# The latent queries' DRAM scratch, split into two tensors: nope rows and rotary rows of all heads

## The chip, the cores and the metric

One NeuronCore of a Trainium2 chip runs the whole kernel in one launch. The metric is device time in microseconds (us) of one execution; lower is better. The program runs on one core, so there is one span and one TensorE clock to look at.

Names of engines: PE is TensorE (PEld its weight loads), DVE is VectorE, ACT is ScalarE, POOL is GpSimd, SP is SyncE. SP computes nothing here: it issues most of the DMAs, strictly in its own order. ACT also issues some DMAs, in between its computing. "SPq" and "ACTq" are these two issuing sequencers.

## The reference, cut to what matters

One layer of an encoder is applied to two groups of tokens (2048 and 512) with the same weights. Only branch B, the latent attention, is touched. Its queries come from a latent vector of 384 values per token and fall into a part without position (nope, 64 values per head) and a rotary part (32 values per head), for 8 heads:

```python
q = (rms_norm(cq, g_q) @ w_uq).reshape(B, S, B_HEADS, NOPE_DIM + ROPE_DIM)
q_nope, q_rope = q[..., :NOPE_DIM], q[..., NOPE_DIM:]
...
q_rope = apply_rope(q_rope, cos[:, None, :], sin[:, None, :])
...
q = jnp.concatenate([q_nope, q_rope], axis=-1) * scale
...
s = jnp.einsum("bqhd,bkhd->bhqk", q_blk, k)
p = jax.nn.softmax(s, axis=-1)
o = jnp.einsum("bhqk,bkhd->bqhd", p, v)
```

Everything is float32. The kernel keeps the precision on TensorE by splitting each value into a high part and a low part, so that each matrix product becomes three matmuls.

## The kernel before, in words

The tokens are cut into NC = 5 chunks of T = 512 (chunks 0 to 3 are the long group, chunk 4 the short one). The program has three stages, and data passes from one to the next through scratch tensors in DRAM.

**Stage one** (to about 590 us) makes, chunk by chunk, all projections that attention needs. In `chunk` (from L376), round a and round b multiply the normed tokens by the weight columns of the latents (tiles `tka`, `tkb`); then four `qa_` steps make the windowed branch's queries, with the transposes of the next chunk's tokens (`pt`, L251) and its `hh` tiles (`h_tile`, ACT at L260, DVE at L257 and L261) between them; then the latents are transposed (`ct`, L491). What makes the latent queries, keys and values of the chunk is the list of closures of `heads` (L300): `qr_`, `kn_`, `qn_`, `v_` four times each, then `qrt_` twice. This list is not run at once: it is kept as `late` and dealt out between the matmuls of rounds a and b of the next chunk. The last chunk's list runs at the end of the stage, with three of its `qa_` steps between.

Each of these steps puts its result into a tile of the tag `ev`, of which there are EV = 6: 128 partitions by 2 (high, low) by 512 values, 512 KB. ACT writes the high half, DVE the low half, then SP stores the tile to DRAM. `qn_` (L328) holds the nope rows of two heads and stores them at L340; `qrt_` (L363) holds the rotary rows of four heads and stores them at L372. Both go to `q_d[c]` (L78), which has for each head 96 rows: 64 nope rows, then 32 rotary rows, each row 4 KB. A `qn` store thus writes two separate blocks of 64 rows, and a `qt` store four separate blocks of 32 rows:

```python
nc.sync.dma_start(q_d[c][2 * j:2 * j + 2, 0:64], f(qn))
...
nc.sync.dma_start(q_d[c][4 * i:4 * i + 4, 64:96], f(qt))
```

An `ev` tile can be written again only when its store has landed. `qa`, `kn`, `vt`, `krt` and `ka` tiles share the six buffers. With its 20 `qn` stores and 10 `qt` stores the kernel writes all of `q_d`. Late in the stage `first_max` (L271) reads back two heads' queries and takes row maxima with the matmuls `mq`, so that the first two items of stage two have theirs already.

**Stage two** (to about 1400 us) is the latent attention. Its 40 items are (head, chunk) pairs, laid out in units of one key block pair by a table (`at`, `run`, from L775); the order on PE, ACT, DVE and POOL is that of the table, while SP's order is set by the tile scheduler. `q_load` (L665) loads an item's 96 rows of queries into one of four `Q` tiles with one DMA (L668). Then the first matmuls `mp` of the item (L677) take its row maxima, and the matmuls `s` (L715 to L717) make its scores. `k_tile`, `load_k` and `load_v` load keys and values.

**Stage three** (to the end) is the windowed attention, the gates and the output projections. It does not read the latent queries.

The order of all instructions in stages one and three, and of SP everywhere, comes from a scheduler that runs when the program is built. A DMA of another shape can therefore move other instructions.

Of the kernel before, what the change touches and what calls it, by code (L numbers as in the profile page):

```python
# [9 lines left out]
F32 = mybir.dt.float32  # L10
# [8 lines left out]
P = 128  # L19
D = 1024  # L20
KD = D // P
T = 512
NS = 4
NC = 5
HA = 8
HB = 8
# [7 lines left out]
def f(ap):  # L34
    return ap.bitcast(F32)
# [3 lines left out]
def encoder(ctx: ExitStack, tc: tile.TileContext, x_prompt, x_sample, c_prompt, c_sample, b_ada, g_norm, g_q,  # L39
            w_uq, g_kv, w_ukv, sink, g_final, t_mod, t_gate, t_col, t_a, t_b, t_oa, t_ob, t_out, rope_c, rope_s, bias, sel, y_prompt, y_sample):  # L40
    nc = tc.nc
# [12 lines left out]
    dram = ctx.enter_context(tc.tile_pool(name="dram", bufs=1, space=DRAM))  # L54
# [5 lines left out]
    def pa(name):  # L60
        return pps["a"].tile([P, 512], F32, name=name, tag="a")

    def px(tag, name):
        return pps["t" if tag == "t0" else "c"].tile([P, 512], F32, name=name, tag=tag)
# [10 lines left out]
    bcol = const.tile([P, 2, KD], F32, name="bcol")  # L75

    h_d = [[dram.tile([P, 2, T], F32, name=f"h_d{c}_{k}") for k in range(KD // 2)] for c in range(NC)]
    q_d = [dram.tile([HB, 96, 2, T], F32, name=f"q_d{c}") for c in range(NC)]  # L78
    k_d = [dram.tile([HB, 64, 2, n * T], F32, name=f"k_d{n}") for n in (NS, 1)]
    kr_d = [dram.tile([32, 2, n * T], F32, name=f"kr_d{n}") for n in (NS, 1)]  # L80
    v_d = [dram.tile([HB, P, 4 * n, P], F32, name=f"v_d{n}") for n in (NS, 1)]
# [16 lines left out]
    def mm3(ps, wh, wl, mh, ml, first, last):  # L98
        nc.tensor.matmul(ps, wh, mh, start=first, stop=False)  # L99
        nc.tensor.matmul(ps, wl, mh, start=False, stop=False)  # L100
        nc.tensor.matmul(ps, wh, ml, start=False, stop=last)  # L101
# [105 lines left out]
    with psum("ps1a", 4) as pps["a"], psum("ps1t", 1) as pps["t"], psum("ps1c", 1) as pps["c"], \  # L207
# [5 lines left out]
        def tl(tag, shape, dt, name, bufs):  # L213
            return p1.tile(shape, dt, name=name, tag=tag, bufs=bufs)

        def tr(tag, shape, dt, name, bufs):
            return env["pl1"].tile(shape, dt, name=name, tag=tag, bufs=bufs)
# [54 lines left out]
        def first_max():  # L272
            K, Q = [], tl("hh", [P, 2, T], F32R, "qm", NH)
            for i in range(2):
                kt = tl("hh", [P, 2, T], F32R, f"km{i}", NH)
                for r0, src in ((0, k_d[0][0]), (64, kr_d[0])):
                    nc.sync.dma_start(f(kt[r0:r0 + src.shape[0]]).rearrange("p a b -> p (a b)"),
                                      src[:, 0, i * 1024:(i + 1) * 1024])
                K.append(kt)
            for c in range(NP):  # L280
                nc.sync.dma_start(f(Q[0:96, c]), q_d[c][0][:, 0, :])
            m0 = [tl("m0", [P, 4, 4], F32, f"m0_{c}", 2) for c in range(NP)]

            def step(c, i):
                ps = px(("t1", "t2", "t3")[i % 3], f"mq{c}_{i}")
                nc.tensor.matmul(ps, Q[0:96, c, i // 4 * P:(i // 4 + 1) * P], K[i % 4 // 2][0:96, i % 2],
                                 start=True, stop=True)
                nc.vector.tensor_reduce(out=m0[c][:, i // 4, i % 4:i % 4 + 1], in_=ps, axis=AX.X, op=ALU.max)

            def close(c):  # L290
                ng = tl("ng", [P, 4], F32, f"ng_{c}", 2)
                nc.vector.tensor_reduce(out=ng, in_=m0[c], axis=AX.X, op=ALU.max, negate=True)
                pt = px("t1", f"mr{c}")
                nc.tensor.transpose(pt[0:4, 0:P], ng, ident)
                rw = tl("rw", [4, P], F32R, f"rw_{c}", 2)
                nc.scalar.copy(rw, pt[0:4, 0:P])
                nc.sync.dma_start(rw_d[c][0], f(rw))

            out = []
            for c in range(NP):  # L300
                out += [lambda c=c, i=i: step(c, i) for i in range(16)] + [lambda c=c: close(c)]
            return out

        def heads(c, C):
            g, cg = c // NS, c % NS
            blk0 = cg * 4
            cs = slice(cg * T, (cg + 1) * T)
            qrs = []

            def ps_of(name):  # L310
                if c == NC - 1:
                    return pa(name)
                env["turn"] = env.get("turn", 0) + 1
                return px(("t0", "t1", "t2", "t3")[env["turn"] % 4], name)

            def ev_of(name):
                return tr("ev", [P, 2, T], F32R, name, EV)

            def qr_(t):
                ts = slice(t * P, (t + 1) * P)  # L320
                ps = ps_of(f"qr{c}_{t}")
                for k in range(3):
                    mm3(ps[:, 0:256], C[k][:, 0, ts], C[k][:, 1, ts], wuh[:, k, 512:768], wul[:, k, 512:768],
                        k == 0, k == 2)
                qs = tr("qs", [P, 8, 32], F32, f"qs{c}_{t}", 1)
                nc.scalar.activation(qs.rearrange("p h e -> p (h e)"), ps[:, 0:256], AF.Copy, scale=SB)
                qr = tr("qrr", [P, 8, 32], F32, f"qr{c}_{t}", 4)
                rope(qr, qs, 8, blk0 + t, f"q{c}_{t}")  # L328
                qrs.append(qr)

            def qn_(j):
                ps = ps_of(f"qn{c}_{j}")
                js = slice(j * P, (j + 1) * P)
                for k in range(3):
                    mm3(ps, wuh[:, k, js], wul[:, k, js], C[k][:, 0, :], C[k][:, 1, :], k == 0, k == 2)
                qn = ev_of(f"qn{c}_{j}")
                nc.scalar.activation(qn[:, 0, :], ps, AF.Copy, scale=SB)
                nc.vector.scalar_tensor_tensor(out=qn[:, 1, :], in0=ps, scalar=SB, in1=f(qn[:, 0, :]),
                                               op0=ALU.mult, op1=ALU.subtract)
                nc.sync.dma_start(q_d[c][2 * j:2 * j + 2, 0:64], f(qn))  # L340

            def kn_(j):
                ps = ps_of(f"kn{c}_{j}")
                js = slice(j * P, (j + 1) * P)
                for k in range(2):
                    mm3(ps, wkh[:, k, js], wkl[:, k, js], C[3 + k][:, 0, :], C[3 + k][:, 1, :], k == 0, k == 1)
                kn = ev_of(f"kn{c}_{j}")
                nc.scalar.copy(kn[:, 0, :], ps)
                nc.vector.tensor_tensor(out=kn[:, 1, :], in0=ps, in1=f(kn[:, 0, :]), op=ALU.subtract)
                nc.sync.dma_start(k_d[g][2 * j:2 * j + 2, :, :, cs], f(kn))  # L350

            def v_(t):
                ts = slice(t * P, (t + 1) * P)
                ps = ps_of(f"v{c}_{t}")
                for k in range(2):
                    mm3(ps, C[3 + k][:, 0, ts], C[3 + k][:, 1, ts], wkh[:, k, 512:1024], wkl[:, k, 512:1024],
                        k == 0, k == 1)
                vt = ev_of(f"vt{c}_{t}").rearrange("p a b -> p (a b)").rearrange("p (h e) -> p h e", h=HB)
                pv = ps.rearrange("p (h e) -> p h e", e=64)
                nc.scalar.copy(vt[:, :, 64:128], pv)  # L360
                nc.vector.tensor_tensor(out=vt[:, :, 0:64], in0=pv, in1=f(vt[:, :, 64:128]), op=ALU.subtract)
                nc.sync.dma_start(v_d[g][:, :, 4 * cg + t, :].rearrange("h p e -> p h e"), f(vt))

            def qrt_(i):
                pt = ps_of(f"qrt{c}_{i}")
                for t in range(4):
                    nc.tensor.transpose(pt[:, t * P:(t + 1) * P],
                                        qrs[t][:, 4 * i:4 * i + 4, :].rearrange("p h e -> p (h e)"), ident)
                qt = ev_of(f"qt{c}_{i}")
                nc.scalar.copy(qt[:, 0, :], pt)  # L370
                nc.vector.tensor_tensor(out=qt[:, 1, :], in0=pt, in1=f(qt[:, 0, :]), op=ALU.subtract)
                nc.sync.dma_start(q_d[c][4 * i:4 * i + 4, 64:96], f(qt))  # L372

            out = []
            for j in range(4):
                out += [(qr_, j), (kn_, j), (qn_, j), (v_, j)]  # L376
            return [lambda fn=fn, j=j: fn(j) for fn, j in out + [(qrt_, 0), (qrt_, 1)]]

        def chunk(c, H, nxt):
# [67 lines left out]
            if c == NC - 1:  # L447
                fm += first_max()
# [190 lines left out]
    with psum("ps2s", 2) as pss, psum("ps2v", 1) as ps2v, psum("ps2", 1) as ps2, pool("p2k") as pk, pool("p2q") as pq, pool("p2a") as p2a, \  # L639
# [25 lines left out]
        def q_load(it):  # L665
            nm = it.nm
            it.Q = pq.tile([97, 2, T], F32R, name=f"Q{nm}", tag="Q", bufs=4)
            nc.sync.dma_start(f(it.Q[0:96]), q_d[it.c][it.h])  # L668
            it.mx = pq.tile([P, 4, 2], F32, name=f"mx{nm}", tag="mx", bufs=5)
            it.ng = pq.tile([P, 4], F32, name=f"ng{nm}", tag="ng", bufs=5)  # L670

# [101 lines left out]
        it = items[0]  # L773
# [335 lines left out]
```

## Time and profile before

| | |
|---|---|
| median of 3 runs | 2773.03 us (2768.88 to 2774.62) |
| the profiled execution's own time | 2767.52 us |
| its span | 2765.6 us |
| mean granted TensorE clock | 0.973 of full speed |
| PE busy | 2589.5 us, 94% of the span |
| DVE, ACT, POOL busy | 61%, 49%, 60% |
| moved by DMA | 392.34 MB, mean 142 GB/s |

The profile shows one execution. In its rows a time is in us from the start of the span, and `x20` means 20 such instructions. "ACT qa L475 <- DMA q_d<-qt" reads: ACT stood still before the instruction at line 475 that writes `qa`, and what let it go was the landing of a DMA from `qt` to `q_d`. A DMA issue (`DMA_DIRECT2D`) on SPq has a duration of its own, the time that it held the issuing sequencer; its data can land much later. "DMA share" is the mean busy share of the core's 16 DMA engines, so that one engine busy all the time counts 0.06.

### The profile page before, as it was taken

How to read it: one execution, taken by the hardware profiler on the slowest of the kernel's cores; microseconds unless marked ns; L12 is line 12 of the kernel's file. 1: busy time of each engine (PE TensorE's matmuls, PEld its weight loads, DVE VectorE, ACT ScalarE, POOL GpSimd, SP SyncE). 2: the span in 40 equal slices, each digit the busy share in tenths (PEclk: the TensorE clock that was granted, in tenths of full speed). 3: DMA queues.
4: the chain of work that ended last, by engine and by line, in shares of the span. 5: the costliest groups of instructions: out<-in, count | busy, mean ns of one | idle time of the engine just before them, and what ended most of it. 6: DMA issues, size and time to landing. Idle time of an engine off the chain costs nothing. (4 is left out here: it accounts for less than half of the span.)

```text
span 2765.6 us, 33922 instructions
## 1 busy us (share of the span) xinstructions
PE 2589.5 (94%) x11842; PEld 2056.5 (74%) x11842; DVE 1691.2 (61%) x2507; ACT 1345.7 (49%) x2125; POOL 1647.4 (60%) x1012
## 2 busy tenths in 40 slices
PE   7998798967999999999899999999999999999998
PEld 4876686745777777777667787787788778778876
DVE  4544443526999999999957466537653754465325
ACT  4534343225777777777654444444344444443422
POOL 3544353316888888888774366436743773467345
PEclk9998899988999999999999999999999999999999
DMA  8557565454322232221245455434543563455341
GB/s 317 183 179 221 181 203 167 143 162 138 91 64 78 71 92 62 84 75 55 82 155 169 136 181 175 149 123 154 195 144 114 180 217 120 137 174 190 107 155 53
DMA packets 198360, 392.34 MB, mean 142 GB/s; under 512 B 17015, under 2 KB 96312, under 8 KB 196587
## 3 DMA queue, kind: packets, MB, share of 16 engines
q1 hardware_dynamic: 185138, 353.31, 39.3%
q10 hardware_dynamic: 13050, 36.86, 4.1%
q8 instruction: 93, 1.52, 0.2%
q14 instruction: 79, 0.64, 0.1%
HBM read 286.52 MB, written 103.58 MB: 141 GB/s over the span
## 5 line engine op out<-in xcount | busy, mean ns | idle before, releaser
L732 POOL TENSOR_TENSOR pl<-pf,ph 128x1024 fp32r<-128x1024 f32 x272 | 655.0, 2412 | 172.4 <-ACT pf L725 172.1
L122 POOL TENSOR_TENSOR wlgm<-wrgm,whgm 128x1024 fp32r<-128x1024 f32 x80 | 195.0, 2443 | 317.9 <-ACT whgm L121 226.0
L724 ACT ACTIVATE ph<-s 128x1024 fp32r<-128x1024 f32 x272 | 278.8, 1025 | 211.7 <-PE s L717 210.7
L683 DVE TENSOR_REDUCE mx<-mp 128x1 f32<-128x1024 f32 x240 | 292.7, 1220 | 56.4 <-PE mp L677 54.4
L745 DVE TENSOR_TENSOR ac<-ac,pf 128x512 f32<-128x512 f32 x424 | 294.2, 694 | 16.5 <-ACT pf L725 9.5
L725 ACT ACTIVATE pf<-s 128x1024 f32<-128x1024 f32 x272 | 275.8, 1014 | 0.0
L100 PE MATMUL gm<-H,wlgm 128*128 128x512 f32 x640 | 252.7, 395 | 0.0
L99 PE MATMUL gm<-H,whgm 128*128 128x512 f32 x640 | 251.8, 397 | 0.0
L101 PE MATMUL gm<-H,whgm 128*128 128x512 f32 x640 | 251.7, 394 | 0.0
L715 PE MATMUL s<-Q,K 97*128 97x512 f32 x544 | 217.6, 400 | 22.4 <-DMA k_d<-kn 22.3
L716 PE MATMUL s<-Q,K 96*128 96x512 f32 x544 | 217.3, 400 | 0.0
L717 PE MATMUL s<-Q,K 96*128 96x512 f32 x544 | 215.8, 397 | 0.0
L677 PE MATMUL mp<-K,Q 96*128 96x512 f32 x512 | 163.1, 400 | 25.3 <-DMA Q<-q_d 17.4
L757 PE MATMUL a<-ph,V 128*128 128x512 f32 x544 | 175.1, 403 | 0.1
L760 PE MATMUL a<-pl,V 128*64 128x512 f32 x544 | 170.7, 395 | 1.0 <-POOL pl L732 0.9
L166 DVE CUSTOM_DVE_ANT_0 S<-as,mask,snk 128x384 f32<-128x384 f32 (+1 forms) x160 | 89.2, 586 | 100.3 <-PE as L164 72.9
L677 PEld LDWEIGHTS mp<-K,Q 96*128 96x128 f32 x512 | 94.1, 190 | 64.8 <-DVE mx L683 18.3
L99 PEld LDWEIGHTS gm<-H,whgm 128*128 128x128 f32 x640 | 119.9, 188 | 25.6 <-issue 2.6
L715 PEld LDWEIGHTS s<-Q,K 97*128 97x128 f32 x544 | 103.4, 190 | 47.9 <-issue 22.5
L101 PEld LDWEIGHTS gm<-H,whgm 128*128 128x128 f32 x640 | 120.8, 189 | 24.5
L100 PEld LDWEIGHTS gm<-H,wlgm 128*128 128x128 f32 x640 | 120.8, 189 | 23.8
L187 DVE TENSOR_TENSOR PT<-pT,PT 128x512 fp32r<-128x512 f32 x112 | 77.1, 688 | 97.9 <-ACT PT L186 96.8
(259 smaller groups left out, 6643.6 us busy)
## 6 DMA issues: line engine op xcount, KB each, us to landing
wrgm<-in_t_col_dram SPq DMA_DIRECT2D x80, 512.0 KB
wrz<-in_t_col_dram SPq DMA_DIRECT2D x40, 512.0 KB
wrw<-in_t_out_dram SPq DMA_DIRECT2D x40, 512.0 KB
Q<-q_d SPq DMA_DIRECT2D x40, 384.0 KB
wrqa<-in_t_col_dram ACTq DMA_DIRECT2D x20, 512.0 KB
qa_d<-qa SPq DMA_DIRECT2D x40, 256.0 KB
k_d<-kn SPq DMA_DIRECT2D x20, 512.0 KB
q_d<-qn SPq DMA_DIRECT2D x20, 512.0 KB
```

What stands on the lines that cost most here:

```text
L99: nc.tensor.matmul(ps, wh, mh, start=first, stop=False)
L100: nc.tensor.matmul(ps, wl, mh, start=False, stop=False)
L101: nc.tensor.matmul(ps, wh, ml, start=False, stop=last)
L677: nc.tensor.matmul(ps[:, j, :], Q[0:96, 0, qt * P:(qt + 1) * P], K[0:96, 0, kc * T:(kc + 1) * T], start=True, stop=True)
L683: nc.vector.tensor_reduce(out=it.mx[:, i // 2, i % 2:i % 2 + 1], in_=it.mp.rearrange("p a b -> p (a b)"), axis=AX.X, op=ALU.max)
L715: nc.tensor.matmul(ps[:, j, :], K[0:97, 0, ks], Q[0:97, 0, :], start=True, stop=False)
L716: nc.tensor.matmul(ps[:, j, :], K[0:96, 1, ks], Q[0:96, 0, :], start=False, stop=False)
L717: nc.tensor.matmul(ps[:, j, :], K[0:96, 0, ks], Q[0:96, 1, :], start=False, stop=True)
L724: nc.scalar.activation(ph, it.s, AF.Exp)
L725: nc.scalar.activation(pf, it.s, AF.Exp)
L732: nc.gpsimd.tensor_tensor(out=pl, in0=it.pf[p], in1=f(it.ph[p]), op=ALU.subtract)
L745: nc.vector.tensor_tensor(out=sm if last and j else it.acc, in0=it.acc, in1=pf[:, j], op=ALU.add)
```

## The change

The scratch tensor `q_d` of each chunk becomes two: `qn_d` has the nope rows of all eight heads (512 rows), `qr_d` the rotary rows of all eight (256 rows). A `qn` store now writes 128 rows that follow each other, and so does a `qt` store. The bytes written and read are the same. The reader now needs two loads where there was one: 64 nope rows and 32 rotary rows, in `q_load` and in `first_max`.

```diff
-    q_d = [dram.tile([HB, 96, 2, T], F32, name=f"q_d{c}") for c in range(NC)]
+    qn_d = [dram.tile([HB * 64, 2, T], F32, name=f"qn_d{c}") for c in range(NC)]
+    qr_d = [dram.tile([HB * 32, 2, T], F32, name=f"qr_d{c}") for c in range(NC)]
...
             for c in range(NP):
-                nc.sync.dma_start(f(Q[0:96, c]), q_d[c][0][:, 0, :])
+                nc.sync.dma_start(f(Q[0:64, c]), qn_d[c][0:64, 0, :])
+                nc.sync.dma_start(f(Q[64:96, c]), qr_d[c][0:32, 0, :])
...
-                nc.sync.dma_start(q_d[c][2 * j:2 * j + 2, 0:64], f(qn))
+                nc.sync.dma_start(qn_d[c][j * P:(j + 1) * P], f(qn))
...
-                nc.sync.dma_start(q_d[c][4 * i:4 * i + 4, 64:96], f(qt))
+                nc.sync.dma_start(qr_d[c][i * P:(i + 1) * P], f(qt))
...
             it.Q = pq.tile([97, 2, T], F32R, name=f"Q{nm}", tag="Q", bufs=4)
-            nc.sync.dma_start(f(it.Q[0:96]), q_d[it.c][it.h])
+            nc.sync.dma_start(f(it.Q[0:64]), qn_d[it.c][it.h * 64:(it.h + 1) * 64])
+            nc.sync.dma_start(f(it.Q[64:96]), qr_d[it.c][it.h * 32:(it.h + 1) * 32])
```

The order of PE's instructions is the same through stages one and two. SP's order is the same in stage one but for the doubled loads. The first place to see is SP at the hand-over from stage one to stage two, where the last stores of chunk 4 and the first loads of keys (`K`) and queries (`Q`) meet (`rw_d` holds the row maxima of `first_max`). Before:

```order
L340 DMA q_d_94<-qn_2_5270 2x64x1024
L362 DMA v_d_100<-vt_2_5281 128x8x128
L647 DMA K_0_5428<-ones_d 1x2048
L649 DMA K_0_5428<-kr_d_97 32x4096
L655 DMA K_0_5428<-k_d_95 64x4096
L668 DMA Q_0_5432<-q_d_90 96x1024
L708 DMA Q_0_5432<-rw_d_136 1x512
```

and with the change:

```order
L342 DMA qn_d_94<-qn_2_5277 128x1024
L364 DMA v_d_105<-vt_2_5288 128x8x128
L649 DMA K_0_5435<-ones_d 1x2048
L651 DMA K_0_5435<-kr_d_102 32x4096
L657 DMA K_0_5435<-k_d_100 64x4096
L670 DMA Q_0_5439<-qn_d_90 64x1024
L671 DMA Q_0_5439<-qr_d_95 32x1024
L711 DMA Q_0_5439<-rw_d_141 1x512
```

The store has another shape (2 blocks of 64 rows became 128 rows), the query load is two rows, and the key loads stand behind the same store as before. The second place is SP in the middle of stage two, at the query load of chunk 3, where a store and a load of row maxima (`rw_d`) of other items stand around it. Before:

```order
L708 DMA Q_1_6115<-rw_d_137 1x512
L668 DMA Q_1_6582<-q_d_93 96x1024
L704 DMA rw_d_140<-rw_1_6493 4x128
L708 DMA Q_1_6319<-rw_d_140 1x512
L747 DMA sm_d_126<-sm_1_6504 128x512
```

and with the change:

```order
L711 DMA Q_1_6128<-rw_d_142 1x512
L670 DMA Q_1_6598<-qn_d_93 64x1024
L707 DMA rw_d_145<-rw_1_6509 4x128
L671 DMA Q_1_6598<-qr_d_98 32x1024
L711 DMA Q_1_6333<-rw_d_145 1x512
L750 DMA sm_d_131<-sm_1_6520 128x512
```

The rotary half of this load now stands behind the `rw_d` store. This is so for six of the forty items, the ones of chunk 3 in heads 1 to 6; in one more (head 0, chunk 4) five loads of keys and values stand between the halves; in the rest the two halves follow each other.

In stage three the scheduler placed a number of instructions in another order on all engines; none was added or taken away there.

## Rows read from the trace of the kernel before

**Rows 1.** The page: part 1, and the clock row of part 2 (40 slices).
```profile
PE 2589.5 (94%) x11842; PEld 2056.5 (74%) x11842; DVE 1691.2 (61%) x2507; ACT 1345.7 (49%) x2125; POOL 1647.4 (60%) x1012
...
PEclk9998899988999999999999999999999999999999
```

**Rows 2.** Windows: stretch, length, busy us of PE, PEld, DVE, ACT, POOL; clock, DMA share, GB/s.
```profile
64.00:142.00 78.00, 77.28 (x422) 66.66 (x423) 48.48 (x82) 43.46 (x85) 46.52 (x69) 1.00 0.63 199
142.00:200.00 58.00, 52.20 (x273) 44.47 (x272) 26.24 (x51) 21.46 (x50) 29.29 (x46) 0.97 0.57 189
200.00:240.00 40.00, 26.34 (x120) 21.31 (x118) 17.95 (x24) 15.42 (x23) 10.19 (x6) 0.79 0.70 228
240.00:300.00 60.00, 60.00 (x335) 52.85 (x334) 20.89 (x45) 24.07 (x54) 35.15 (x57) 1.00 0.56 180
300.00:350.00 50.00, 34.03 (x159) 27.56 (x158) 26.03 (x35) 19.74 (x30) 12.47 (x16) 0.83 0.64 204
...
405.00:465.00 60.00, 49.68 (x228) 39.25 (x227) 27.62 (x43) 21.60 (x41) 19.67 (x34) 0.91 0.55 175
465.00:589.00 124.00, 114.32 (x564) 93.81 (x562) 57.41 (x104) 38.22 (x83) 48.15 (x89) 0.96 0.47 149
589.00:650.00 61.00, 20.34 (x67) 14.49 (x67) 11.14 (x16) 14.93 (x17) 14.60 (x6) 0.64 0.63 179
```

**Rows 3.** Waits of PE, 110 to 660 us: total us, times, longest us.
```profile
PE ct L491 <- ACT hh L260: 22.7, 5, 13.9
PE s L715 <- DMA k_d<-kn: 22.3, 1, 22.3
PE mp L677 <- DMA Q<-q_d: 17.4, 1, 17.4
```

**Rows 4.** Waits of ACT, 110 to 625 us: total us, times, longest us.
```profile
ACT qa L475 <- DMA q_d<-qt: 25.8, 2, 14.3
ACT qt L370 <- DMA q_d<-qn: 24.2, 3, 9.8
...
ACT qa L475 <- DMA q_d<-qn: 17.3, 2, 9.8
```

**Rows 5.** Timeline of SP's DMA issues, from 281 us: start us, duration us.
```profile
281.29 0.52 SPq L340 DMA_DIRECT2D q_d<-qn  x1
281.90 3.49 SPq L362 DMA_DIRECT2D v_d<-vt  x1
285.49 11.85 SPq L350 DMA_DIRECT2D k_d<-kn  x1
```

**Rows 6.** Windows: behind `qt` stores, behind a `qn` store, and at the start.
```profile
200.00:206.00 6.00, 6.00 (x32) 5.02 (x31) 1.25 (x2) 0.00 (x0) 0.62 (x1) 1.00 0.24 90
...
618.00:624.00 6.00, 5.15 (x22) 3.43 (x21) 3.40 (x5) 4.11 (x6) 6.00 (x4) 1.00 0.13 53
0.00:22.00 22.00, 10.08 (x63) 4.86 (x64) 7.09 (x20) 8.45 (x14) 5.37 (x11) 1.00 0.92 357
```

**Rows 7.** Windows: five stretches of low clock; the first, and the sum of all.
```profile
212.48:229.55 17.07, 6.66 (x23) 5.28 (x24) 10.97 (x14) 10.02 (x15) 6.78 (x3) 0.50 0.75 221
...
sum 85.33, PE 26.05 PEld 20.00 DVE 26.29 ACT 23.36 POOL 15.89; mean PE 5.21 PEld 4.00 DVE 5.26 ACT 4.67 POOL 3.18
```

**Rows 8.** Timeline of SP and of PE: two query loads and the first `mp` of each.
```profile
630.70 0.40 SPq L668 DMA_DIRECT2D Q<-q_d  x1
...
644.45 1.22 PE L677 MATMUL mp<-K,Q 96*128 96x512 f32 x2 [17.42 <-DMA Q<-q_d]
...
727.22 0.31 SPq L668 DMA_DIRECT2D Q<-q_d  x1
...
751.02 0.63 PE L677 MATMUL mp<-K,Q 96*128 96x512 f32 x2
```

**Rows 9.** Waits in 660 to 1400 us: the longest of PE, and one of SP.
```profile
PE mp L677 <- DVE mx L683: 7.8, 2, 7.5
...
SPq L704 <- ACT rw L703: 183.2, 28, 14.5
```

## The prediction

> **What bounds the kernel now.** The page comes first: PE is busy 94% of the span and no other engine comes near it [rows 1]. So the time is PE's work plus the stretches in which PE stands still or runs at a low clock. The clock row has its low digits in the first quarter of the span (one slice is 69 us) and hardly any after it [rows 1]. The second view is the windows over that quarter, cut where PE's load changes [rows 2]. In chunk 0's stretch, 64 to 142 us, PE is busy 77.28 of 78 us, and in 240 to 300 us all of the time. In between stand five stretches with idle time: 5.8 + 13.7 = 19.5 us in 142 to 240, 16.0 in 300 to 350, 10.3 in 405 to 465, 9.7 in 465 to 589 and 40.7 in 589 to 650. Together that is 96.2 us. The whole span has 2765.6 - 2589.5 = 176 us of idle PE, so over half of it lies here.
>
> The third view is who is waited for. PE's longest waits are at `ct` for ACT's `hh` (22.7 us in total) and, at the hand-over to attention, twice for a DMA: 22.3 us before the first scores and 17.4 us before the first `mp` [rows 3]. So in the middle of stage one PE waits for ACT. For what does ACT wait? For stores of queries to land: before `qa` 25.8 us on `qt` stores and 17.3 us on `qn` stores, before `qt` another 24.2 us on `qn` stores [rows 4]. These are waits for an `ev` tile. ACT works in order, so the `hh` behind the blocked `qa` comes late, and then PE's transposes.
>
> Why do the stores land late? SP's timeline shows it [rows 5]. SP gets rid of a `qn` store in 0.52 us, but then the next issues hold it for 3.49 and 11.85 us. The windows in such times show a DMA share of 0.13 and 53 GB/s behind a `qn` store, and 0.24 and 90 GB/s behind `qt` stores [rows 6]. Of 16 engines, 0.13 is two and 0.24 is four: as many as the store has blocks of rows. At 53 GB/s the 512 KB of a `qn` store take 9.9 us, at 90 GB/s those of a `qt` store 5.8 us. All the while most DMA engines do nothing, and SP, with the key and query loads behind it, stands.
>
> **The change, part by part.**
>
> *The 20 `qn` and 10 `qt` stores become 128 rows in one piece.* The trace of before has no such store, so I bound its time: above by today's 9.9 us, below by tiles of 128 rows of 4 KB loaded at the start of the program at 357 GB/s [rows 6], 1.5 us. These are loads, and stage one has other traffic, so I take 3 us, near the lower end because the shape is the same. The round of issues in [rows 5] lasts 0.52 + 3.49 + 11.85 = 15.9 us, nearly all of it held up, and there are six `ev` tiles, so at 3 us a store no writer should wait for a tile. SP is then no longer held.
>
> What this gives, stretch by stretch [rows 2]. In chunk 0's stretch the same kind of work runs (round b, four `qa` steps, transposes and `hh` of the next chunk) without any query stores before it, and PE idles 0.7 us. That is my model for the later chunks. Of 19.5 us in 142 to 240 I leave 2, and of 16.0 us in 300 to 350 I leave 1.5. In 405 to 465 ACT's large waits on query stores are not seen, so I credit half and leave 5 of 10.3. In 465 to 589 PE's idle time is in small pieces beside the row maxima of `first_max`; I leave 8 of 9.7. At the hand-over I leave 5 of 40.7: by the shapes in SP's order the first keys (32 and 64 rows of 4096 values) and two query loads (96 rows of 1024) are 2.3 MB, 6.6 us at 357 GB/s, and part of it passes before PE is done with stage one, since SP is no longer late. The second wait there goes too: this query load was issued at 630.70 us, behind two `qt` stores, and its `mp` began at 644.45 [rows 8]. Sum: 96.2 - 21.5 = 74.7 us.
>
> *The clock.* Around these gaps the granted clock fell to 0.50, which is 1.2 of 2.4 GHz, each time after PE had stood still; in five such stretches PE was busy 26.05 us [rows 7]. At full clock that work takes at best half, so up to 13.0 us come back. I take 10, since some gaps stay.
>
> *40 query loads, and 2 in `first_max`, become two each.* One issue costs SP 0.31 us [rows 8], so 42 more cost 13 us of SP. The work that hides it is the attention itself: in 660 to 1400 us PE's longest wait on anything is 7.5 us, on DVE, while SP stands 183.2 us waiting for ACT's row copies alone [rows 9]. A typical load is issued at 727.22 and its `mp` starts at 751.02 [rows 8], a lead of 23.8 us. Should that cover go, each late us costs up to 38 times (items with `mp`). For the seven items whose rotary half stands behind other DMAs, the longest wait for `rw` is 14.5 us [rows 9], which still leaves 9.3 of the lead. I cost it at nothing.
>
> Here a page speaks against the change. The Trainium skill, "DMA: Bandwidth & Descriptors", section "Rules for kernel authors", says not to use two transfers for disjoint groups of partitions, as they run on the same engines one after the other, but one; its section "Anatomy of one DMA" gives a fixed cost of about 2.0 us per DMA (for the GpSimd path). By that, if it were exposed, an estimate of 38 x 2.0 = 76 us would be lost and the sum would end near 2764 instead of 2688. No run here shows the fixed cost for such a half; the lead of 23.8 us would hide it.
>
> *Stage three* has some instructions in another order. Of 176 us of idle PE, 80 lie outside the stretches above; I cost the new order at nothing and allow 10 us each way, an eighth of that.
>
> **Sum.** 2767.5 (the profiled execution) - 74.7 - 10 = 2682.8. The median shown is 5.5 us above that execution, so the prediction is 2688 us. A measurement of this kernel can tell about 0.2%, 5.5 us, from no change.
>
> **The rivals.**
>
> *Only the hand-over gains.* The stalls in the chunks stay, because the next thing takes the place of the query stores: the `qa` stores share the six `ev` tiles, and there is much traffic (228 GB/s in 200 to 240 us [rows 2]), which spread-out stores now meet on all engines. Against it stands chunk 0's stretch with the same `qa` stores and PE at 77.28 of 78. It would give 35.7 us of the hand-over and some 4 of the clock (two of the five stretches): 2773 - 40 = 2733.
>
> *The store does not get faster.* It might be slow for its 4 KB rows or for where they land, not for its two blocks. Then nothing moves: 2773. Against it: the share of 0.13 is two engines working without a pause, and 0.24 four. By the Trainium skill's same page, section "Why a DMA increments its semaphore by 16 and not by 1", a DMA gets the largest number of engines up to 16 that divides the slowest dimension of both sides, which is 2, 4 and now 16. The trace's shares agree for 2 and 4.
>
> *Slower: the second half of the queries comes late.* The place is the wait before each `mp` in stage two. PE pays if a pair of loads lands later than 23.8 us after its issue; it eats the gain of 85 us when 38 items are each late by 2.2 us, a landing of 26.0 us. The worst landing seen is at most 13.74 us (630.70 to 644.45 [rows 8]), behind clogged engines; at twice that, 27.5 us, it would cost 38 x 3.7 = 141 us and end at 2829. For it: one load more in SP's order, and seven halves behind a wait.
>
> **How the numbers follow.** My forecast gets 0.66, only the hand-over 0.26, no faster store 0.04, late queries 0.04. The range: at the low end all 96.2 us and 13.0 us of clock come back, 2773 - 109 = 2664; at the high end the hand-over alone, 2733, with 2 of the allowance for stage three, 2735. Leaving out the last two rivals and some misses inside, about 2 in 10 lie outside. Faster by over 0.2%: 0.92; within 0.2%: 0.04; slower: 0.04.
>
> **What would show it.** Right: no window in stage one with a DMA share near 0.13 while SP is held; SP's issues after a `qn` store under 1 us or a few; no ACT waits on `qn_d` or `qr_d` of more than some us in total; PE's waits at `ct` below 5 us; the wait before the first `s` below 8 us and before the first `mp` near nothing; the clock at 1.00 from about 65 us on, but for short dips. Wrong: if ACT's waits at `qa` turn to `qa_d` or `h_d` stores of the same size, the first rival holds; if the share of 0.13 stays, the second; if PE waits at `mp` for `qn_d` or `qr_d` in stage two, the third. If stage three differs by more than 10 us, my allowance for its order was too small.

## The result, and the profile after

The changed kernel takes 2673.75 us (median of 4 runs, 2669.64 to 2683.87) against 2770.95 us (2765.64 to 2774.62) before, a ratio of 0.966 with a 95% interval of 0.962 to 0.969. The prediction was 2688 us in a range of 2664 to 2735: right in sign, size and place, and 14 us too cautious. Its profiled execution took 2669.64 us, with a span of 2666.4 us. These are the two rows of the page that answer to [rows 1], part 1 and the clock:

```profile
PE 2579.6 (97%) x11842; PEld 2049.1 (77%) x11842; DVE 1698.3 (64%) x2507; ACT 1344.4 (50%) x2125; POOL 1649.8 (62%) x1012
...
PEclk9999999899999999999999999999999999999999
```

PE is busy 97% instead of 94% of the span. Its busy time fell by 9.9 us (2589.5 to 2579.6) with the same number of matmuls: the clock accounts for it, whose low digits in the first quarter are gone but for one; the amount is rough, since a1 and e1 below, both at a clock of 0.988, have PE busy 2582.1 and 2573.4 us. Its idle time fell by 89.3 us, from 176.1 to 86.8. The two together are the 99.2 us by which the span became shorter.

The windows that answer to [rows 2] (stretch, length, busy us of PE, PEld, DVE, ACT, POOL, then clock, DMA share and GB/s): chunk 0's stretch, the rest of stage one in two pieces, and the hand-over.

```profile
64.00:142.00 78.00, 77.25 (x422) 66.34 (x421) 47.08 (x83) 43.47 (x87) 45.90 (x68) 1.00 0.65 206
142.00:405.00 263.00, 260.97 (x1395) 224.60 (x1393) 138.21 (x231) 121.74 (x237) 136.99 (x195) 1.00 0.74 235
405.00:526.00 121.00, 116.64 (x575) 96.96 (x574) 60.51 (x108) 42.40 (x90) 49.14 (x89) 0.94 0.57 173
526.00:560.00 34.00, 29.01 (x112) 21.40 (x111) 19.81 (x24) 21.09 (x24) 22.30 (x10) 0.90 1.04 291
```

Chunk 0's stretch is as it was. Behind it PE now idles 2.0, 4.4 and 5.0 us, 11.4 us where there were 96.2 [rows 2]. The DMA engines work at a share of 0.74 and 235 GB/s where much the same traffic had run at 0.55 to 0.70.

SP's issues around a `qn` store, to set beside [rows 5] (start us, duration us):

```profile
258.54 0.53 SPq L352 DMA_DIRECT2D k_d<-kn  x1
262.21 0.32 SPq L342 DMA_DIRECT2D qn_d<-qn  x1
266.77 0.37 SPq L364 DMA_DIRECT2D v_d<-vt  x1
268.78 0.32 SPq L374 DMA_DIRECT2D qr_d<-qt  x1
```

No issue behind the store is held: the `v` store takes 0.37 us instead of 3.49, and between the issues SP stands idle. In the stretch 262 to 272 us, which has a `qn` and a `qt` store in it, the share is 0.67:

```profile
262.00:272.00 10.00, 10.00 (x73) 9.47 (x72) 4.16 (x12) 5.58 (x17) 6.13 (x14) 1.00 0.67 196
```

The waits that answer to [rows 3] and [rows 4], first PE's two longest in 110 to 660 us, then ACT's longest for DMAs in 110 to 625 us (total us, times, longest):

```profile
PE s L718 <- DMA Q<-qr_d: 3.2, 1, 3.2
PE mp L680 <- DMA Q<-qr_d: 1.7, 1, 1.7
```

```profile
ACT kn L350 <- DMA wrqa<-in_t_col_dram: 7.3, 2, 3.6
ACT vt L362 <- DMA qm<-qn_d: 1.7, 1, 1.7
```

Of 22.3 and 17.4 us at the hand-over, 3.2 and 1.7 are left. No writer waits for a query store any more (`qm<-qn_d` is a load of `first_max`).

The split loads stay hidden, as [rows 8] said of the lead. Here is the load whose rotary half stands behind the `rw_d` store, and the `mp` that reads it, from the timelines of SP and of PE:

```profile
747.71 0.47 SPq L670 DMA_DIRECT2D Q<-qn_d  x1
748.27 0.43 SPq L707 DMA_DIRECT2D rw_d<-rw  x1
748.75 0.31 SPq L671 DMA_DIRECT2D Q<-qr_d  x1
```

```profile
771.48 0.64 PE L680 MATMUL mp<-K,Q 96*128 96x512 f32 x2
```

The second half is issued 1.04 us after the first and 22.7 us before it is needed.

### The profile page after: what moved, and what is told of

Read it like the earlier page. It is cut to its first block, busy times and chain, and to the rows that moved or that the text cites. A ratio compares the mean times of both kernels' runs of the same rounds, so it can differ in the third digit from the quotient of the medians.

```text
span 2666.4 us, 33977 instructions
## 1 busy us (share of the span) xinstructions
PE 2579.6 (97%) x11842; PEld 2049.1 (77%) x11842; DVE 1698.3 (64%) x2507; ACT 1344.4 (50%) x2125; POOL 1649.8 (62%) x1012
## 5 line engine op out<-in xcount | busy, mean ns | idle before, releaser
L748 DVE TENSOR_TENSOR ac<-ac,pf 128x512 f32<-128x512 f32 x424 | 294.2, 694 | 16.5 <-ACT pf L728 9.6
L947 DVE SCALAR_TENSOR_TENSOR G<-G,po 128x512 f32<-128x512 f32 x80 | 53.5, 684 | 126.7 <-PE po L102 103.2
L102 PE MATMUL out<-wlw,M 128*128 128x512 f32 x320 | 124.3, 398 | 6.1 <-POOL wlw L123 6.0
```

Of the source, the lines that this page charges most:

```text
L748: nc.vector.tensor_tensor(out=sm if last and j else it.acc, in0=it.acc, in1=pf[:, j], op=ALU.add)
```

## The experiments

The theory: a store runs on as many DMA engines as its outermost dimension allows. With 2 blocks it sits on two engines, with 4 on four; while it drains, SP is held, and whatever shares those engines comes late. The main rivals: two tensors or neighbouring rows are what counts; only the `qn` stores or only the `qt` stores count; the second load costs something. Each experiment was timed against the kernel before on the same chip (medians 2763 us for the first four, 2766 for the others).

One table first. Idle PE is read from two windows of each run, from 142 us to the end of stage one's last matmul, and from there to a few us past the first `mp`. These are the rows of the kernel before (its second is in [rows 2]) and of the changed one:

```profile
142.00:589.00 447.00, 391.58 (x1966) 327.23 (x1964) 194.54 (x338) 162.70 (x324) 184.43 (x283) 0.94 0.56 179
...
142.00:526.00 384.00, 377.61 (x1968) 321.56 (x1967) 198.72 (x339) 164.14 (x326) 186.13 (x284) 0.98 0.69 215
526.00:552.00 26.00, 21.01 (x78) 15.34 (x77) 12.32 (x17) 14.84 (x18) 15.43 (x7) 0.87 1.05 294
```

| run | ratio to before (95% interval) | idle PE, stage one from 142 us | idle PE, hand-over |
|---|---|---|---|
| before | 1 | 55.4 | 40.7 |
| changed | 0.9656 (0.9624 to 0.9688) | 6.4 | 5.0 |
| a1_changed_again | 0.9673 (0.9652 to 0.9694) | 6.7 | 5.4 |
| e1_one_tensor | 0.9688 (0.9672 to 0.9704) | 7.3 | 6.9 |
| e2_spare_row | 1.0051 (1.0034 to 1.0068) | 50.8 | 39.5 |
| e3_qn_one_piece | 0.9714 (0.9699 to 0.9729) | 6.7 | 13.5 |
| e4_qt_one_piece | 0.9918 (0.9903 to 0.9933) | 32.1 | 31.2 |
| e6_qn_four_blocks | 0.9755 (0.9740 to 0.9771) | 7.8 | 24.4 |
| e7_stores_from_pool | 0.9776 (0.9760 to 0.9792) | 18.8 | 19.2 |
| e8_four_buffers | 0.9681 (0.9666 to 0.9695) | 6.9 | 11.6 |

**e1_one_tensor.** The scratch of before, the load of before, but one store for each head:

```diff
-                nc.sync.dma_start(q_d[c][2 * j:2 * j + 2, 0:64], f(qn))
+                for u in range(2):
+                    nc.sync.dma_start(q_d[c][2 * j + u, 0:64], f(qn[u * 64:(u + 1) * 64]))
...
-                nc.sync.dma_start(q_d[c][4 * i:4 * i + 4, 64:96], f(qt))
+                for u in range(4):
+                    nc.sync.dma_start(q_d[c][4 * i + u, 64:96], f(qt[u * 32:(u + 1) * 32]))
```

> The kernel before with its one scratch tensor and its one query load per item, but each qn store is issued as two stores of 64 rows (one head each) and each qt store as four of 32 rows. Theory (a store runs on as many DMA engines as its outermost dimension allows, so 2 blocks hold it to two engines and 4 blocks to four): every store now has 64 or 32 rows outermost, so the time is that of the changed kernel, 2674 within 10 us, with no share of 0.13 in the windows and no ACT waits on q_d. Rival (the split into two tensors, or rows of all heads lying together in DRAM, is what made the store fast): the time stays at 2771 within 8 us and the waits of ACT on q_d stay at some 70 us. Rival (the second half load of each item costs something): faster than the changed kernel by over 5 us.

Measured: 2675.26 us, as fast as the changed kernel. The two windows:

```profile
142.00:525.00 383.00, 375.72 (x1964) 320.18 (x1963) 199.28 (x339) 163.68 (x326) 184.77 (x282) 0.99 0.72 215
525.00:553.00 28.00, 21.08 (x76) 15.51 (x77) 12.14 (x18) 14.62 (x17) 15.89 (x7) 0.88 1.02 274
```

The addresses written are exactly those of before. So neither the second tensor nor where the rows lie matters; the shape of one store does. Some waits of ACT for `q_d` are left, 9.1 us in two, and PE does not feel them. And as this kernel has one load per item and is not faster than the changed one, the second load costs nothing that can be measured.

**e2_spare_row.** The changed kernel with one unused row behind each head's rows, so that the 128 rows of a store fall into blocks again (the loads take the same rows as in the changed kernel):

```diff
-    qn_d = [dram.tile([HB * 64, 2, T], F32, name=f"qn_d{c}") for c in range(NC)]
-    qr_d = [dram.tile([HB * 32, 2, T], F32, name=f"qr_d{c}") for c in range(NC)]
+    qn_d = [dram.tile([HB, 65, 2, T], F32, name=f"qn_d{c}") for c in range(NC)]
+    qr_d = [dram.tile([HB, 33, 2, T], F32, name=f"qr_d{c}") for c in range(NC)]
...
-                nc.sync.dma_start(qn_d[c][j * P:(j + 1) * P], f(qn))
+                nc.sync.dma_start(qn_d[c][2 * j:2 * j + 2, 0:64], f(qn))
...
-                nc.sync.dma_start(qr_d[c][i * P:(i + 1) * P], f(qt))
+                nc.sync.dma_start(qr_d[c][4 * i:4 * i + 4, 0:32], f(qt))
```

> The changed kernel with its two tensors and two loads, but with one unused row of DRAM behind each head's rows, so that a qn store is again 2 blocks of 64 rows and a qt store 4 blocks of 32 rows. PE's order is that of the changed kernel throughout, stage three too. Theory (number of blocks): the loss comes back, 2771 within 10 us, share 0.13 behind a qn store and 0.24 behind qt stores. Rival (two tensors are what counts): 2674 within 10 us. What stage three's new order is worth shows here too: stage two and three should last as long as in the changed kernel, within 5 us.

Measured: 2777.24 us; the whole gain is gone. The windows, the second with a stretch of low share inside it, and two of ACT's waits (total us, times, longest):

```profile
142.00:584.00 442.00, 391.19 (x1956) 327.83 (x1954) 193.92 (x336) 160.80 (x322) 181.99 (x280) 0.93 0.57 180
584.00:644.00 60.00, 20.51 (x65) 14.76 (x65) 10.90 (x15) 13.77 (x17) 14.61 (x6) 0.64 0.63 166
614.00:620.00 6.00, 6.00 (x27) 4.47 (x26) 3.29 (x6) 4.46 (x5) 6.00 (x3) 1.00 0.16 59
```

```profile
ACT qt L372 <- DMA qn_d<-qn: 26.0, 4, 10.0
...
ACT qa L477 <- DMA qr_d<-qt: 23.9, 2, 14.4
```

One row of 4 KB between two heads brings back the gaps, the low clock (0.93 in stage one, 0.94 before), a share of 0.16 in 614 to 620 us (0.13 before [rows 6]) and these two of ACT's waits of [rows 4] nearly to the number. The order of PE's instructions is that of the changed kernel here, in stage three too, so the new order has no part in the gain: from the last `s` to the end stage three takes 1354.0 us here, 1352.2 in the changed kernel, 1350.1 before. That this kernel is 0.5% slower than before is not explained: its profiled execution, its fastest run, does not show where the 14 us go.

**e3_qn_one_piece** and **e4_qt_one_piece.** One half of the change each: the spare row behind the rotary rows alone, or behind the nope rows alone.

> The changed kernel with only the qn stores in one piece; each qt store is again 4 blocks of 32 rows (a spare row behind each head's rotary rows). Theory: a qt store takes 5.8 us on four engines, two come back to back in each chunk, 10 in all; SP is held for up to 11 us a chunk and ACT waits for them before qa (25.8 us in the kernel before), so some 15 to 35 us of the 97 are lost again: 2690 to 2710. Rival (only the 2-block stores matter): 2674 within 8 us.

> The changed kernel with only the qt stores in one piece; each qn store is again 2 blocks of 64 rows (a spare row behind each head's nope rows). Theory: 20 stores of 9.9 us hold SP and their ev tiles as before; 60 to 85 us of the 97 are lost again: 2735 to 2760, and the share of 0.13 is back. Rival (the pairs of qt stores did the harm): 2674 to 2700.

Measured: 2684.25 us and 2739.83 us. First e3, its third row from a time in which `qt` stores drain, then e4:

```profile
142.00:524.00 382.00, 375.31 (x1957) 319.71 (x1955) 196.09 (x337) 161.96 (x323) 183.39 (x280) 0.98 0.68 215
524.00:558.00 34.00, 20.55 (x66) 14.97 (x67) 10.31 (x15) 13.67 (x16) 14.61 (x6) 0.75 0.77 224
541.00:544.00 3.00, 2.27 (x10) 1.30 (x8) 1.46 (x3) 2.57 (x4) 3.00 (x2) 1.00 0.25 104
```

```profile
142.00:561.00 419.00, 386.91 (x1958) 325.30 (x1956) 193.18 (x337) 161.67 (x322) 182.70 (x280) 0.96 0.59 190
561.00:613.00 52.00, 20.80 (x68) 15.22 (x68) 10.79 (x15) 14.23 (x16) 14.59 (x6) 0.67 0.72 193
```

With the `qt` stores alone in blocks (e3) the chunks are free of gaps and 8.5 us come back at the hand-over; the time lies between the two expectations (2690 to 2710, and up to 2682). The share of 0.25 at 104 GB/s in 541 to 544 us is four engines, all of it in SP's queue. With the `qn` stores alone (e4) 25.7 us come back in stage one and 26.2 at the hand-over, and the time is as the theory expected. The two halves do not add up: 0.3 + 25.7 is 26 us of idle time in stage one, but with both (e2) it is 44.4. So the `qt` stores in blocks do most of their harm together with the `qn` stores; that they hurt where they queue up behind them is the likely reason, not tested by itself. In the kernel before, ACT's wait for `qt` stores was the largest line for a store, 25.8 us [rows 4], and taken alone that reading is wrong by a lot: in e4, where a `qt` store is in one piece, ACT still waits 12.5 us for one.

**a1_changed_again** repeats the changed kernel beside the last three experiments:

> The changed kernel unaltered, so that the runs beside it can be set against it on one chip. All theories: a ratio to the kernel before of 0.962 to 0.971.

Measured: 2675.3 us, as expected.

**e6_qn_four_blocks.** A `qn` store as 4 blocks of 32 rows, with the loads cut to match:

```diff
-    qn_d = [dram.tile([HB * 64, 2, T], F32, name=f"qn_d{c}") for c in range(NC)]
+    qn_d = [dram.tile([HB * 2, 33, 2, T], F32, name=f"qn_d{c}") for c in range(NC)]
...
-                nc.sync.dma_start(qn_d[c][j * P:(j + 1) * P], f(qn))
+                nc.sync.dma_start(qn_d[c][4 * j:4 * j + 4, 0:32], f(qn))
...
-            nc.sync.dma_start(f(it.Q[0:64]), qn_d[it.c][it.h * 64:(it.h + 1) * 64])
+            for u in range(2):
+                nc.sync.dma_start(f(it.Q[u * 32:(u + 1) * 32]), qn_d[it.c][2 * it.h + u, 0:32])
```

> The changed kernel with each qn store as 4 blocks of 32 rows (a spare row behind every 32), and each query load as three loads of 32 rows. Theory (time of a store goes with the number of blocks, and it hurts once a round of stores is longer than PE's work beside it): a qn store runs on four engines at 90 GB/s, 5.8 us, inside a round of some 13 us, so most of the harm is gone: ratio to the kernel before 0.966 to 0.980. Rival (any blocks in a store do the full harm): 0.99 to 1.005. Rival (more loads per item cost stage two something): over 0.980 with stage two longer by over 10 us than in the changed kernel, at equal gaps in stage one.

Measured: 2699.36 us, inside the theory's range. The windows, SP's issues at the hand-over, and the issue of the kernel before that answers to the last of them:

```profile
142.00:524.00 382.00, 374.20 (x1955) 318.15 (x1953) 195.19 (x336) 160.99 (x321) 182.75 (x280) 0.99 0.67 209
524.00:569.00 45.00, 20.60 (x67) 14.72 (x66) 10.90 (x15) 13.95 (x17) 14.62 (x6) 0.70 0.81 213
```

```profile
518.65 0.56 SPq L343 DMA_DIRECT2D qn_d<-qn  x1
519.31 1.15 SPq L365 DMA_DIRECT2D v_d<-vt  x1
520.57 5.29 SPq L650 DMA_DIRECT2D K<-ones_d  x1
...
587.10 8.37 SPq L647 DMA_DIRECT2D K<-ones_d  x1
```

With four blocks instead of two the store does next to no harm in stage one (7.8 us idle against 6.4), but SP is still held for 5.29 us at the very issue that held it for 8.37 us before, and the hand-over idles 24.4 us. So the same store is judged twice: between chunks it only has to drain within a round of PE's work, at the hand-over a backlog adds to PE's waits. That second part my expectation had not named. How much of it is the store is open, as each item has three query loads here, at the hand-over too. The rival on loads is not borne out: stage two takes 770.1 us against 762.2 in the changed kernel, under the 10 us that it named, and e3 with two loads takes 768.7.

**e7_stores_from_pool.** The kernel before, with the same blocked stores issued by GpSimd (`nc.gpsimd.dma_start`), so that SP's queue does not hold them.

> The kernel before with its qn and qt stores issued by GpSimd instead of SP, blocks as before. SP is not held by them any more, but they still land late. Theory 1 (two harms: tiles that come free late stall ACT in the chunks; SP held back delays the hand-over): the hand-over's 39.7 us of idle PE shrink to under 20, ACT's waits for the stores in the chunks stay over 30 us; ratio 0.975 to 0.992. Rival 2 (all harm comes through SP's queue): ratio 0.970 or less. Rival 3 (all harm comes through late landing and busy engines): within 0.5% of the kernel before.

Measured: 2705.15 us. The windows, and ACT's waits for the stores; then the stores' time from issue to landing, and SP's issues of `k_d` stores (ns, shortest, median and longest) here and in the kernel before:

```profile
142.00:540.00 398.00, 379.22 (x1952) 320.85 (x1952) 194.68 (x337) 160.60 (x321) 206.75 (x308) 0.97 0.69 204
540.00:582.00 42.00, 22.84 (x81) 17.07 (x79) 12.76 (x18) 15.52 (x18) 18.18 (x10) 0.72 0.92 225
```

```profile
ACT kn L348 <- DMA q_d<-qn: 14.2, 1, 14.2
ACT qa L475 <- DMA q_d<-qn: 10.9, 1, 10.9
ACT qt L370 <- DMA q_d<-qn: 9.4, 2, 5.1
ACT vt L360 <- DMA q_d<-qn: 6.8, 1, 6.8
```

```profile
DMA to landing us min/median/max: 11.8/17.4/23.5
L350 SPq DMA_DIRECT2D k_d<-kn x20: 348/543/3954, 138.4 to 547.8; - x20
...
L350 SPq DMA_DIRECT2D k_d<-kn x20: 343/3922/11912, 141.2 to 604.2; - x20
```

Both harms exist, as theory 1 said, but the split is not the one I had in mind. The stores still land late, a median of 17.4 us after their issue, and ACT still waits 41.3 us for them, yet stage one's idle time falls from 55.4 to 18.8 us: SP is held no longer, its `k_d` issues take 0.54 us (median) instead of 3.92. So in the chunks, too, most of the damage went with the stores in SP's queue, where every other store waits behind the blocked one and its `ev` tile with it. How exact this split is was not shown: a store in GpSimd's queue does not wait behind SP's other stores either, and whether it runs on the same engines as from SP was not tested. The hand-over halves to 19.2 us: the first query load is issued at 534.0 us, before stage one's last matmul, but the first `s` starts only at 553.4, after 13.0 us of waiting for that load. What lands late there is no longer SP's delay; that the engines are still busy with blocked stores is the likely reason, not a shown one.

**e8_four_buffers.** The changed kernel with four `ev` tiles:

```diff
-        NR, NW, EV = 3, 3, 6
+        NR, NW, EV = 3, 3, 4
```

> The changed kernel with four ev tiles instead of six. Theory (with stores that land in some 3 us the writers need few buffers): ACT's waits for stores rise to some 10 to 30 us, PE's idle time in stage one by under 10 us, ratio to the kernel before 0.965 to 0.975. Rival (six buffers are needed even with fast stores): over 0.98. The scheduler places some of stage one's matmuls in another order here, so up to 5 us either way may come from that.

Measured: 2676.9 us, no difference from a1 that the intervals show. PE idles 6.6 us more at the hand-over, and stage one is as with six tiles (6.9 us idle). With fast stores four tiles do; of slow stores this says nothing. More than six in the kernel before, which would have tested the tiles from the other side, was not tried.

## Why the prediction was right, point by point

**What bounds the kernel** was read rightly: PE, plus five stretches. Nearly all of the time came from those, none from stage three, which takes 1352.2 us against 1350.1 before.

**The store.** That the shape of one store decides is shown by e1 (same addresses, other shape, fast), e2 (one row between heads, slow) and e6 (four blocks, in between). "As many engines as the store has blocks" rests on the shares: 0.13 for two blocks [rows 6] and 0.25 for four (e3). The row of 0.24 that I read as four engines was less clean than I took it for: in 200 to 206 us SP's queue had 19.5% and ACT's queue 4.7%. The Trainium skill, "DMA: Bandwidth & Descriptors", section "Why a DMA increments its semaphore by 16 and not by 1", states it as a rule: the largest number of engines up to 16 that divides the slowest dimension of both sides. These runs agree with it for 2 and 4; of stores of 32, 64 and 128 rows they show that SP is not held behind them. How long the new store takes by itself (I took 3 us) no run measured.

**The sum.** The stretches were to keep 21.5 us of idle PE; they kept 11.4. Stage one from 142 us on was to keep 16.5 and kept 6.4: the term that I had sized too carefully, above all "in 405 to 465 I credit half" and "I leave 8 of 9.7". I had halved the first because the rows did not name a query store there. ACT's longest waits in 405 to 465 us of the kernel before are these:

```profile
ACT qa L475 <- DMA h_d<-h: 12.4, 2, 10.3
...
ACT qa L475 <- issue: 9.0, 1, 9.0
```

ACT issues the `h_d` stores itself, so they do not stand in SP's queue; in the changed kernel ACT waits for none of them. That they came late because they shared engines with blocked query stores is likely, not tested. A wait is written down under the name of what came last, which need not be the culprit's. The hand-over was to keep 5 us and kept 5.0 (526 to 560 us). The clock was to give 10 us, and PE's busy time fell by 9.9. That these two came out to a tenth is luck: the hand-over keeps 6.9 us in e1, as fast a kernel, and PE's busy time differs by 8.7 us between a1 and e1. Outside the stretches another 4.5 us of idle time went, within the 10 allowed for stage three and the like.

**The mechanism in the chunks** is the step that the runs correct in part. I put the chunk gaps down to ACT waiting for an `ev` tile whose own store drains slowly, with SP's delay as the hand-over's matter. In e7, with stores that drain slowly but do not hold SP, 12.4 us of idle time are left above the changed kernel's (18.8 - 6.4), of 49.0 (55.4 - 6.4) before; the other 36.6 went with SP's queue, as far as e7 separates the two. The waits for `h_d` stores are a third way, which neither I nor an experiment singled out. The number came out because all of these go when the store is fast, so the sum did not depend on the split.

**The rivals.** "Only the hand-over gains" fell: no wait on `qa_d` or `h_d` stores took the place of the query stores. "The store does not get faster" fell with the result. "The second half comes late" fell twice: the longest wait for a half load is 3.2 us, at the hand-over, and e1 with whole loads is not faster. The rule of the Trainium skill against two transfers to disjoint halves of the partitions ("DMA: Bandwidth & Descriptors", "Rules for kernel authors") had no price here that could be measured; a lead such as the 22.7 us above covers the second DMA.

## What to carry to other kernels

Look at the shape of a DMA as it is issued, not only at its bytes: if the outermost dimension on the DRAM side is 2 or 4, make the rows one piece, or issue one DMA per block, which was as fast here and changed no layout. In a profile the sign is a DMA share that sits at 1/8 or 1/4 while the issuing queue is held for 10 us at a time. What it costs is less the transfer itself than what is queued behind it, so the waits in the list can carry other names than the culprit's, such as the 22.3 us for `k_d<-kn` [rows 3]. An experiment that moves the suspect to another queue shows how much of the harm goes with the queue.

## What the runs showed of the hardware that was not expected

In [rows 5] a blocked store holds the issuing sequencer at later issues and not at its own: 0.52 us for the store, then 3.49 and 11.85 us for the next two. With the same stores issued by GpSimd, SP's `k_d` issues took a median of 0.54 us instead of 3.92 (e7), though ACT still waited 41.3 us for the stores to land. And `qn` stores of four blocks, all but harmless in stage one, still went with 24.4 us of idle PE at the hand-over (e6), where key and query loads queue behind them.
